# Planner costs, the places of twelve gates and one-bank accumulators in a two-layer hybrid backbone

## The chip, the core and the metric

One core of a Trainium2 chip runs the whole program: TensorE (PE, with its weight loads PEld), VectorE (DVE), ScalarE (ACT), GpSimd (POOL), and SyncE (SP), which issues the DMAs. The metric is the device time of one execution, in microseconds (us). All arithmetic that the result rests on is float32 or float32r; every large product is made of three float32r products.

## What is computed

The reference, cut to the parts that the change touches:

```python
for l in range(DEPTH):                                    # 2 layers, D_MODEL 1024
    h  = rms_norm(x)   * (1 + scale)   + shift            # 512 latent tokens
    hc = rms_norm(ctx) * (1 + scale_c) + shift_c          # 256 context tokens
    # one input projection feeds three mixers and the gates mg (3 x 1024 columns)
    y_gla  = head_norm_gate(bidir_recurrence(gla),  ga_g) # 4 heads, chunked scans
    y_hg   = head_norm_gate(bidir_recurrence(hgrn), hg_g) # 8 heads, chunked scans
    y_att  = window_attention(q, k, v, sink) * silu(wa_g) # 8 query heads, 2 kv heads
    merged = sum_n sigmoid(mg[n]) * (y[n] @ w_branch[n])  # n = gla, hg, att
    x      = x + gate * (merged @ w_out)
    # in layer 1 the context tokens go the same way; in layer 2 they only give k, v and states
return rms_norm(x)
```

## The kernel before

Tokens lie along the free dimension: 768 columns (512 latent, then 256 context), 128 channels to a tile. `hH` and `hL` hold the rounded and the remaining part of the normalised input. A **projection** (`proj_T`) takes one 128-column block of weights and makes 24 matmuls of 512 columns and, where context tokens are wanted, 24 of 256 into one accumulator; after its last matmul the caller evicts the accumulator (a copy, a SiLU, a sigmoid, a product). Accumulators come from a pool of two tiles of [128, 1024] floats, two banks each; small products use four one-bank tiles `mx`. `proj_V` makes token-major products, 6 groups of 24 matmuls of 256 columns, three groups to a tile.

Weights: `W` blocks are loaded by SP into three `raw` buffers, split into two parts by ACT or DVE into the ring `wring` (three blocks), up to two blocks ahead.

**What sets the order.** Each engine's order is written out by the program itself. `make_plan` lists the jobs: for each layer the GLA projections, the HGRN projections (`hf`, `hq`, `hg`, `hv`), the attention projections (`av`, `ak`, `aq`, `ag`), then the merge: gates `mg` (n, d), branch products `br` (n, d) and the output `out`. Between the matmuls of these jobs, at `pace()`, the recorder `Emit` fits in steps of **background generators**: `rec_head` (one head of a recurrence: scans on DVE, exps on ACT, transposes and small products on PE), `att_block` (scores, softmax, transposes, products for a block of 128 queries), `rope` and `yload_` (loads the finished rows `y` of a branch back from memory and splits them for `br`). `Emit` keeps a clock per engine from a cost formula per operation (`tt`, `stt`, `scan`, `act`, `copy`, ...) and a hop from engine to engine; `first` puts a step in when the clock says that its inputs are ready no later than 50 ns after PE's place, and `pace` goes on until DVE's or ACT's clock is 3 us ahead of PE's. `need` puts steps in until one generator is done, ready or not. `ACTIVE` bounds how many large generators of a kind are open; before, a generator that could not begin stopped all behind it in the queue (`runnable`).

A gate that is made early (`mgx`) is stored to memory and loaded again at `yneed`, just before its `br`. In layer 1 two gates are made early, in layer 2 eight (four ahead of the attention projections, two each in its third and fourth round).

The loads of `yload_`, of the weights and of early gates, and the stores of all outputs stand in one queue, SP's, in the order written.

The last job before the merge's first product is `yneed (0, ...)`: it loads the early gates and calls `need` for the two `yload_` generators of branch 0, each of four rows: three loads, the first split, the fourth load, three more splits.

## Time and profile before

| what | value |
| --- | --- |
| median of 3 runs (lowest to highest) | 2675.74 us (2675.12 to 2677.64) |
| the profiled execution, its own time | 2677.51 us |
| its span, first to last instruction | 2675.7 us |
| mean granted TensorE clock | 0.995 |
| PE busy | 2607.5 us, 97% |
| DVE, ACT, POOL busy | 1767.0, 1104.8, 169.3 us |
| PE idle (span less busy) | 68.2 us |

How to read it: PE works nearly all the time, so a gain is idle time of PE that goes away, or matmuls that run at the higher clock instead of the lower. Layer 1 goes from 0 to 1515 us (start to 55, GLA to 302, HGRN to 747, attention to 1035, merge from there), layer 2 from 1515 to the end (GLA to 1743, HGRN to 2106, attention to 2379, merge from there). In the rows below, `mx` and `acc` are PSUM tiles, `s` any of 40 slots, `s<-y` a load of a branch's rows, `y<-s` a store of them. The kernel's lines are named as L533 (matmul), L549 (transpose), L439 (activation), L450 (two-tensor operation), L470 (scan), L481 (copy on ACT).

### The profile page before, as it was taken

To read this page: it belongs to the slowest core of one execution; us is meant where nothing else is said; L and a number is where in the kernel's file an instruction comes from. 1 tells how busy PE (TensorE), PEld (TensorE's weight loads), DVE (VectorE), ACT (ScalarE), POOL (GpSimd) and SP (SyncE) were. 2 spreads that over 40 slices of the span, in tenths; PEclk is the share of its full clock that TensorE was granted. 3 is DMA by queue.
4 is the path that set the end of the run, shared out by engine and by line. 5 is a ranking of instruction groups with operands and counts; after the bars stand their busy time and mean duration, and the time that the engine had idled before them with its cause. 6 is when DMAs were issued, how large, how long until landed. Compare 5 with 4: busy or idle time off the path is not lost. (4 is left out here: it accounts for less than half of the span.)

```text
span 2675.7 us, 40576 instructions
## 1 busy us (share of the span) xinstructions
PE 2607.5 (97%) x15982; PEld 2314.4 (86%) x15982; DVE 1767.0 (66%) x3595; ACT 1104.8 (41%) x2034; POOL 169.3 (6%) x426
## 2 busy tenths in 40 slices
PE   8999999999999999999999999999999999999998
PEld 5999989989888888888888798888889797888886
DVE  5566657686777766774546556667887787664454
ACT  4444433444434455321211444445565545663222
POOL 0000002101010100000000000001011110000000
PEclk9999999999999999999999999999999999999999
DMA  7111211111111112553423311112121212224333
GB/s 262 56 52 60 60 60 50 58 46 62 50 53 49 54 58 76 173 193 95 142 95 105 132 50 61 65 62 64 61 68 60 76 56 78 70 93 137 132 124 106
DMA packets 89342, 227.68 MB, mean 85 GB/s; under 512 B 9920, under 2 KB 30912, under 8 KB 89152
## 3 DMA queue, kind: packets, MB, share of 16 engines
q1 hardware_dynamic: 89152, 225.09, 25.6%
q8 instruction: 126, 2.06, 0.3%
q14 instruction: 64, 0.52, 0.1%
HBM read 202.24 MB, written 22.81 MB: 84 GB/s over the span
## 5 line engine op out<-in xcount | busy, mean ns | idle before, releaser
L533 PE MATMUL acc<-hH,wring 128*128 128x512 f32 (+1 forms) x5040 | 1398.8, 356 | 14.6 <-ACT s L439 9.6
L533 PEld LDWEIGHTS acc<-hH,wring 128*128 128x128 f32 x5040 | 894.7, 189 | 141.5 <-ACT s L439 11.3
L533 PE MATMUL acc<-hL,wring 128*128 128x512 f32 (+1 forms) x2520 | 881.6, 351 | 3.6 <-DVE hL L466 3.5
L533 PEld LDWEIGHTS acc<-hL,wring 128*128 128x128 f32 x2520 | 477.2, 190 | 61.9 <-DVE hL L466 5.9
L533 PE MATMUL mx<-s,s 128*128 128x256 f32 (+4 forms) x2576 | 390.0, 299 | 12.8 <-DVE s L513 4.3
L533 PEld LDWEIGHTS mx<-s,s 128*128 128x128 f32 (+1 forms) x2576 | 348.9, 192 | 32.6 <-issue 7.0
L450 DVE TENSOR_TENSOR wring<-raw,wring 128x1024 fp32r<-128x1024 f32 x269 | 330.5, 1234 | 29.2 <-ACT wring L481 19.5
L533 PE MATMUL acc<-s,wring 128*128 128x512 f32 (+1 forms) x1728 | 332.3, 354 | 0.5 <-DVE s L450 0.5
L533 PEld LDWEIGHTS acc<-s,wring 128*128 128x128 f32 x1728 | 285.6, 189 | 46.3 <-DVE s L450 0.9
L439 ACT ACTIVATE s<-s 128x768 f32<-128x768 f32 (+1 forms) x321 | 259.0, 816 | 130.7 <-DVE s L466 83.1
L481 ACT CAST wring<-raw 128x1024 fp32r<-128x1024 f32 x173 | 179.7, 1047 | 276.9 <-PE acc L533 189.9
L533 PE MATMUL acc<-wring,hH 128*128 128x256 f32 x1536 | 286.1, 285 | 0.0
L450 DVE TENSOR_TENSOR s<-s,s 128x768 f32<-128x768 f32 (+5 forms) x279 | 234.2, 854 | 66.7 <-ACT s L439 46.5
L533 PEld LDWEIGHTS acc<-wring,hH 128*128 128x128 f32 x1536 | 242.2, 192 | 0.3
L533 PE MATMUL acc<-wring,hL 128*128 128x256 f32 x768 | 217.2, 283 | 0.0
L450 DVE TENSOR_TENSOR s<-s,fb 128x128 f32<-128x128 f32 (+2 forms) x608 | 182.8, 359 | 0.8
L439 ACT ACTIVATE s<-acc 128x768 f32<-128x768 f32 (+2 forms) x112 | 76.2, 683 | 254.5 <-PE acc L533 234.8
L481 ACT COPY s<-mx 128x256 f32<-128x256 f32 (+2 forms) x187 | 66.2, 379 | 207.4 <-PE mx L533 142.7
L479 DVE CAST wring<-raw 128x1024 fp32r<-128x1024 f32 x103 | 71.5, 694 | 118.0 <-PE acc L533 114.9
L533 PEld LDWEIGHTS acc<-wring,hL 128*128 128x128 f32 x768 | 147.3, 192 | 0.2
L481 ACT COPY s<-acc 128x768 f32<-128x768 f32 (+2 forms) x129 | 87.8, 680 | 98.2 <-PE acc L533 96.1
L549 PE MATMUL mx<-const,s 128*128 128x128 f32 (+1 forms) x732 | 109.6, 276 | 15.7 <-DVE s L450 14.6
(112 smaller groups left out, 2141.8 us busy)
## 6 DMA issues: line engine op xcount, KB each, us to landing
raw<-in_W SPq DMA_DIRECT2D x308, 512.0 KB, 3.8
y<-s SPq DMA_DIRECT2D x80, 128.0 KB, 1.7
s<-y SPq DMA_DIRECT2D x24, 384.0 KB, 6.2
s<-in_xT SPq DMA_DIRECT2D x16, 384.0 KB, 4.0
s<-in_wada SPq DMA_DIRECT2D x16, 384.0 KB, 7.5
s<-y SPq DMA_DIRECT2D x24, 256.0 KB, 4.4
y<-s SPq DMA_DIRECT2D x80, 64.0 KB, 1.6
s<-in_wvl SPq DMA_DIRECT2D x8, 288.0 KB, 6.1
```

Of the source, the lines that this page charges most:

```text
L439: self.nc.scalar.activation(out, in_, func, **kw)
L450: (self.nc.vector if e == 'v' else self.nc.gpsimd).tensor_tensor(out, a, b, op=op)
L479: self.nc.vector.tensor_copy(out, in_)
L481: self.nc.scalar.copy(out, in_)
L533: self.nc.tensor.matmul(out, lhsT=lhsT, rhs=rhs, start=start, stop=stop)
L549: self.nc.tensor.transpose(out, in_, ident)
```

## The change

1. **Costs of `Emit`.** A scan costs 2.05 n + 64 ns for n columns instead of 1.04 n + 65. An operation on DVE with a column operand costs 65 ns more. ACT's fixed part goes from 95 (70 for a copy) to 60 (50) from PSUM and 110 (90) from SBUF, and 90 more with a column as bias or scale. POOL's fixed part goes from 100 to 140.
2. **Accumulators.** The pool holds four tiles of [128, 512], one bank each. `proj_T` and `proj_V` take a tile for each part (512 latent, 256 context) and call an `evac` function inside, as soon as the part's last matmul is written, ahead of the last `pace()`. So each eviction with context becomes two.
3. **Gates.** `AT` and `EARLY` place the early gates. Layer 1: two, as before. Layer 2: twelve, namely (0, 0) to (0, 7) and (2, 7) to (2, 4): three inside HGRN (ahead of its rounds 2, 3, 4), four ahead of attention, four in its third and fourth round, one behind it.
4. **Queue.** In `runnable` a `yload_` that cannot begin no longer stops the others, nor they it; `box` is keyed by row.

```diff
+AT = (((0, 0, 0, 0), 0, (0, 0, 1, 1), 0), ((0, 1, 1, 1), 4, (0, 0, 2, 2), 1))
+EARLY = ([(0, d) for d in range(8)], [(0, d) for d in range(8)] + [(2, 7 - d) for d in range(8)])
...
+    def act_cost(self, out, in_, bias=None, scale=None):
+        return 0.833 * self.size(out) + (60 if self.psum(in_) else 110) + 90 * (self.is_ap(bias) or self.is_ap(scale))
...
-        self._do('a', 0.833 * self.size(out) + 95 + (90 if accum_out is not None else 0), out, [in_, bias, scale])
+        self._do('a', self.act_cost(out, in_, bias, scale) + (90 if accum_out is not None else 0), out, [in_, bias, scale])
...
         self.nc.vector.tensor_tensor_scan(out, d0, d1, 0.0, op0=ALU.mult, op1=ALU.add)
-        self._do('v', 1.04 * self.size(out) + 65, out, [d0, d1])
+        self._do('v', 2.05 * self.size(out) + 64, out, [d0, d1])
...
-    acc_p = es.enter_context(tc.tile_pool(name="acc", bufs=2, space=PSUM))
+    acc_p = es.enter_context(tc.tile_pool(name="acc", bufs=4, space=PSUM))
...
     def runnable():
         out = []
+        held = set()
         for b in queue:
-            if b.running:
+            if b.running or not b.begun and (b.name == 'y') in held:
                 continue
             if not b.begun:
-                if (b.need < 3 or sum(x.need > 2 for x in arena.active) < ACTIVE[b.name]) and \
-                        arena.spare() >= b.need - len(b.own):
-                    out.append(b)
-                break
+                held.add(b.name == 'y')
+                if b.need > 2 and sum(x.need > 2 for x in arena.active) >= ACTIVE[b.name] or \
+                        arena.spare() < b.need - len(b.own):
+                    continue
             out.append(b)
         return out
...
-    def proj_T(i, xH, xL, ctx, m=P):
-
-        ps = acc()
+    PARTS = ((0, NL), (NL, NC))
+
+    def proj_T(i, xH, xL, ctx, evac):
+
         E.t['pe'] = max(E.t['pe'], wready[i])
-        for t0, n in ((0, NL), (NL, NC)) if ctx else ((0, NL),):
+        for t0, n in PARTS[:2 if ctx else 1]:
+            ps = acc()[:, 0:n]
+            sl = slice(t0, t0 + n)
             k = 0
             for kt in range(KT):
                 for w, x in ((WH(i), xH), (WH(i), xL), (WL(i), xH)):
-                    mm(ps[0:m, t0:t0 + n], w[:, kt, 0:m], x[kt][:, t0:t0 + n],
-                       start=(k == 0), stop=(k == 3 * KT - 1))
+                    mm(ps, w[:, kt], x[kt][:, sl], start=(k == 0), stop=(k == 3 * KT - 1))
                     k += 1
                 if kt == 1 and t0 == 0:
                     ahead()
+                if kt == KT - 1:
+                    evac(sl, ps)
                 if kt % 2 == 1:
                     pace()
         pace()
-        return ps
```

Both programs hold 14,829 matmuls, of the same shapes; ACT's instructions go from 1,772 to 1,988, among them table loads from 104 to 147 and reads of PSUM from 784 to 939; DVE's go from 3,597 to 3,579, SP's DMAs from 620 to 628.

**Place 1, PE, layer 2, the third GLA head's V projection and the K projection after it.** The rows with `wring` ahead of `hH` are the V projection, those with `hH` ahead of `wring` the K projection; `mx<-const` are transposes of a head's decayed keys, which DVE makes. Before:

```order
L533 MATMUL acc_15069<-wring_85,hL7_84 128x256
L533 MATMUL acc_15069<-wring_85,hH7_76 128x256
L549 MATMUL mx_15156<-const_90,s767_15126 128x128 x3
L549 MATMUL mx_15161<-const_90,s767_15126 128x128 x2
L533 MATMUL acc_15167<-hH0_69,wring_85 128x512
```

Now (the rows left out are the same three for the second and third `hH`, `hL`):

```order
L552 MATMUL acc_15367<-wring_85,hL7_84 128x256
L552 MATMUL acc_15367<-wring_85,hH7_76 128x256
L552 MATMUL acc_15441<-hH0_69,wring_85 128x512
L552 MATMUL acc_15441<-hL0_77,wring_85 128x512
L552 MATMUL acc_15441<-hH0_69,wring_85 128x512
...
L552 MATMUL acc_15441<-hH3_72,wring_85 128x512
L552 MATMUL acc_15441<-hL3_80,wring_85 128x512
L552 MATMUL acc_15441<-hH3_72,wring_85 128x512
L568 MATMUL mx_15458<-const_90,s767_15434 128x128 x3
L568 MATMUL mx_15463<-const_90,s767_15434 128x128 x2
```

The transposes moved behind twelve matmuls of 512 columns.

**Place 2, SP, the end of layer 1's attention.** `y0_0_k` are the rows of branch 0 that the merge's first product needs, `y0_2_k` outputs of attention blocks, `raw` weights. Before, these stand in the job of the gate (0, 5), with the gates (0, 6) and (0, 7) still to come:

```order
L397 DMA s572_10634<-y0_0_3_157 128x768
L407 DMA y0_2_6_176<-s577_10657 128x128
L407 DMA y0_2_7_177<-s577_10657 128x128
L407 DMA y0_2_6_176<-s578_10669 128x128
L407 DMA y0_2_7_177<-s578_10669 128x128
L397 DMA s581_10684<-y0_0_4_158 128x768
L397 DMA s582_10686<-y0_0_5_159 128x768
```

Now they stand behind the last gate, in `yneed`:

```order
L423 DMA y0_2_6_176<-s572_10961 128x128
L423 DMA y0_2_7_177<-s572_10961 128x128
L413 DMA s573_10966<-y0_0_0_154 128x768
L413 DMA s574_10968<-y0_0_1_155 128x768
L413 DMA s575_10970<-y0_0_2_156 128x768
L413 DMA s578_10976<-y0_0_3_157 128x768
L423 DMA y0_2_6_176<-s587_11006 128x128
L423 DMA y0_2_7_177<-s587_11006 128x128
L413 DMA s588_11011<-y0_0_4_158 128x768
L413 DMA s589_11013<-y0_0_5_159 128x768
L413 DMA s590_11015<-y0_0_6_160 128x768
L413 DMA s593_11021<-y0_0_7_161 128x768
```

All eight loads moved behind the outputs of the last but one attention block, and four of them behind that of the last.

On PE the same place reads so now (`mx<-const` are the last block's transposes, `mx<-s585` its product, `acc<-s576` the merge's first product):

```order
L552 MATMUL mx_10945<-s564_10873,s336_7233 128x256
L568 MATMUL mx_10990<-const_90,s568_10919 128x128
L568 MATMUL mx_10990<-const_90,s569_10922 128x128
L568 MATMUL mx_10990<-const_90,s568_10919 128x128
L568 MATMUL mx_10990<-const_90,s569_10922 128x128
L552 MATMUL mx_10999<-s585_10995,s334_7231 128x256
L552 MATMUL mx_10999<-s586_10996,s334_7231 128x256
...
L552 MATMUL acc_11041<-s576_10972,wring_85 128x512
L552 MATMUL acc_11041<-s577_10973,wring_85 128x512
L552 MATMUL acc_11041<-s576_10972,wring_85 128x512
```

No matmul of a gate is left between the last attention block and the merge's first product.

**Place 3, ACT, layer 1, the gate (0, 0) in the middle of attention.** `sm<-nsink` and the activations of 256 columns beside it are a softmax. Before:

```order
L439 ACT_TABLE_LOAD
L439 ACTIVATE s_9065<-acc 128x768
L481 CAST wring<-raw_8755 128x1024
L481 CAST s_9085<-mx 128x512
L421 ACT_TABLE_LOAD
L439 ACTIVATE sm<-nsink,sm 128x1
```

Now:

```order
L458 ACT_TABLE_LOAD
L458 ACTIVATE s_9017<-acc 128x512
L437 ACT_TABLE_LOAD
L458 ACTIVATE sm<-nsink,sm 128x1
L458 ACTIVATE s_9042,sm<-mx,sm 128x256 x2
L458 ACTIVATE sm<-nsink,sm 128x1
L458 ACTIVATE s_9046,sm<-mx,sm 128x256 x2
L458 ACTIVATE s_9046<-s_9046,sm 128x512
L458 ACT_TABLE_LOAD
L458 ACTIVATE s_9017<-acc 128x256
L437 ACT_TABLE_LOAD
```

The gate's eviction moved apart into two, with a softmax and two table loads between them.

## Rows read from the trace of the kernel before

**Rows 1.** Page, part 1: busy us, share of the span, instructions.
```profile
PE 2607.5 (97%) x15982; PEld 2314.4 (86%) x15982; DVE 1767.0 (66%) x3595; ACT 1104.8 (41%) x2034; POOL 169.3 (6%) x426
```

**Rows 2.** Stretches of the span: busy us of each engine (instructions), clock, DMA, GB/s.
```profile
0.00:100.00 100.00, 89.54 (x592) 70.19 (x593) 52.12 (x110) 43.23 (x66) 0.20 (x4) 0.98 0.53 191
...
1000.00:1100.00 100.00, 98.89 (x662) 89.64 (x659) 62.68 (x143) 54.86 (x123) 0.00 (x0) 1.00 0.30 96
...
2100.00:2200.00 100.00, 96.25 (x639) 86.72 (x638) 80.17 (x199) 44.49 (x98) 12.18 (x35) 0.98 0.20 65
...
2600.00:2700.00 100.00, 64.91 (x282) 52.47 (x280) 37.04 (x49) 15.64 (x19) 0.00 (x0) 0.96 0.23 79
```

**Rows 3.** Waits of PE on accumulators: us in total, times, longest.
```profile
PE acc L533 <- ACT s L439: 9.6, 5, 3.9
...
PE acc L533 <- ACT s L481: 3.0, 2, 1.6
...
PE acc L533 <- DVE s L466: 1.8, 1, 1.8
```

**Rows 4.** PE groups by shape: busy us, mean ns, idle before them, what ended it.
```profile
L533 PE MATMUL mx<-s,s 128*128 128x256 f32 x1200 | 200.5, 317 | 2.2 <-ACT s L439 1.6 <-DVE s L450 0.6
L533 PE MATMUL mx<-s,s 128*128 128x128 f32 x1248 | 162.1, 277 | 10.5 <-DVE s L513 4.3 <-DVE s L479 3.4 <-ACT s L481 2.7
L549 PE MATMUL mx<-const,s 128*128 128x128 f32 x720 | 108.0, 276 | 15.7 <-DVE s L450 14.6 <-ACT s L439 0.5 <-DVE s L462 0.5
```

**Rows 5.** Timeline, DVE and PE, third GLA head of layer 2: start, us, instruction, count.
```profile
1631.11 3.52 DVE L470 TENSOR_TENSOR_SCAN s<-scm,s 128x384 f32<-128x384 f32 x4
...
1645.07 0.74 PE L549 MATMUL mx<-const,s 128*128 128x128 f32 x5 [1.56 <-DVE s L450]
```

**Rows 6.** Timeline, ACT and PE, layer 2's attention, two SiLU evictions behind a softmax.
```profile
2256.31 0.29 ACT L439 ACTIVATE sm<-nsink,sm 128x1 f32<-128x1 f32 x1 [8.57 <-DVE sm L450]
...
2260.15 1.28 ACT L439 ACT_TABLE_LOAD   x1
2261.44 1.09 ACT L439 ACTIVATE s<-acc 128x512 f32<-128x512 f32 x2
...
2262.09 0.50 PE L533 MATMUL acc<-hH,wring 128*128 128x512 f32 x1 [3.94 <-ACT s L439]
```

**Rows 7.** Short stretches of PE: us, busy (matmuls), granted clock, DMA.
```profile
2262.64:2266.06 3.42, 3.42 (x13) 0.50 0.45 153
2266.06:2269.48 3.42, 3.42 (x26) 1.00 0.09 23
...
2444.34:2449.78 5.44, 5.44 (x25) 1.00 0.97 347
```

**Rows 8.** Timeline, end of layer 1's attention: SP's DMAs, splits on ACT and DVE, PE.
```profile
1082.77 1.93 SPq L397 DMA_DIRECT2D s<-y  x4
1091.60 1.74 SPq L407 DMA_DIRECT2D y<-s  x4
1093.44 1.79 SPq L397 DMA_DIRECT2D s<-y  x4
...
1087.13 0.83 ACT L481 CAST s<-s 128x768 fp32r<-128x768 f32 x1 [1.20 <-DMA s<-y]
...
1096.47 0.83 ACT L481 CAST s<-s 128x768 fp32r<-128x768 f32 x1 [5.16 <-DMA s<-y]
...
1092.08 0.94 DVE L450 TENSOR_TENSOR s<-s,s 128x768 fp32r<-128x768 f32 x1
...
1103.19 0.95 DVE L450 TENSOR_TENSOR s<-s,s 128x768 fp32r<-128x768 f32 x1
...
1101.13 0.50 PE L533 MATMUL acc<-hH,wring 128*128 128x512 f32 x1 [2.25 <-ACT s L439]
```

**Rows 9.** ACT's groups: table loads of one of two lines; splits of weights.
```profile
L439 ACT ACT_TABLE_LOAD x53 | 68.0, 1283 | 5.0 <-PE acc L533 3.4 <-PEq L1846 0.7
...
L481 ACT CAST wring<-raw 128x1024 fp32r<-128x1024 f32 x173 | 179.7, 1047 | 276.9 <-PE acc L533 189.9
```

More of the change, by code (lines that the diff above doesn't have):

```diff
@@ L115, in make_plan @@
             job(l, 'grun', h)
+        early = EARLY[l][:sum(sum(x) if isinstance(x, tuple) else x for x in AT[l])]
+        spilled = set(early)
         for p in range(4):
+            for _ in range(AT[l][0][p]):
+                mgx(l, early.pop(0))
             todo = []
@@ L127, in make_plan @@
             job(l, 'hrun', p)
-        early = [(0, d) for d in range(2 if ctx else 8)]
-        spilled = set(early)
-        if not ctx:
-            for _ in range(4):
-                mgx(l, early.pop(0))
+        for _ in range(AT[l][1]):
+            mgx(l, early.pop(0))
         v = False
@@ L144, in make_plan @@
                 job(l, 'aq', h, win('wa_q', h))
-            for _ in range(0 if p < 2 else 1 if ctx else 2):
+            for _ in range(AT[l][2][p]):
                 mgx(l, early.pop(0))
@@ L149, in make_plan @@
             job(l, 'arun', p)
+        for _ in range(AT[l][3]):
+            mgx(l, early.pop(0))
+        assert not early
         cond = [(l, i) for i in range(16, 24)] + [(l + 1, i) for i in range(24)] if ctx else []
@@ L487, in affine @@
         n = self.size(out)
-        cost = {'v': (1.04 if psum else 0.52) * n + 65, 'a': 0.833 * n + 95}
+        cost = {'v': (1.04 if psum else 0.52) * n + 130, 'a': self.act_cost(out, in_, bias)}
         e = self._pick({k: c for k, c in cost.items() if k in eng}, out, [in_])
@@ L496, in scale @@
         n = self.size(out)
-        cost = {'v': 0.52 * n + 65, 'a': 0.833 * n + 95}
+        cost = {'v': 0.52 * n + 130, 'a': self.act_cost(out, in_, None, s)}
         if self._pick({k: c for k, c in cost.items() if k in eng}, out, [in_, s]) == 'v':
@@ L1212, in logsig_gla, with rope, evac @@
         return bg(rest(), 1, 'sig', soon=True)
-    def rope(ps, H, L, ctx, factor=None):
-        w, u = arena.alloc(NL), arena.alloc(NL)
-        for g in range(0, P, 32):
-            copy(u.ap[g ^ 32:(g ^ 32) + 32], ps[g:g + 32, 0:NL], eng='va', psum=True)
-        if factor is None:
-            tt(w.ap, ps[:, 0:NL], cosT, ALU.mult)
-        else:
-            stt(w.ap, ps[:, 0:NL], factor, cosT, ALU.mult, ALU.mult)
-        if ctx and factor is None:
-            E.split(H[:, NL:NT], L[:, NL:NT], ps[:, NL:NT], psum=True)
-        elif ctx:
-            act(H[:, NL:NT], ps[:, NL:NT], AF.Copy, scale=factor)
-            stt(L[:, NL:NT], ps[:, NL:NT], factor, H[:, NL:NT].bitcast(F32), ALU.mult, ALU.subtract)
+    def rope(ctx, factor=None):
+        i = take()
+        n = NT if ctx else NL
+        got = []
+        def evac(sl, ps):
+            if sl.start == 0:
+                got.extend([arena.alloc(n, True), arena.alloc(n, True), arena.alloc(NL), arena.alloc(NL)])
+                w, u = got[2:]
+                for g in range(0, P, 32):
+                    copy(u.ap[g ^ 32:(g ^ 32) + 32], ps[g:g + 32], eng='va', psum=True)
+                if factor is None:
+                    tt(w.ap, ps, cosT, ALU.mult)
+                else:
+                    stt(w.ap, ps, factor, cosT, ALU.mult, ALU.mult)
+            elif factor is None:
+                E.split(got[0].r[:, sl], got[1].r[:, sl], ps, psum=True)
+            else:
+                act(got[0].r[:, sl], ps, AF.Copy, scale=factor)
+                stt(got[1].r[:, sl], ps, factor, got[0].ap[:, sl], ALU.mult, ALU.subtract)
+        proj_T(i, hH, hL, ctx, evac)
+        a, b, w, u = got
+        H, L = a.r, b.r
         def rest():
@@ L1336, in att_block, with project, evac @@
         finish()
-    def silu_evac(ps, n):
-        b = arena.alloc(n)
-        act(b.ap, ps[:, 0:n], AF.Silu)
-        return b
+    def project(ctx, func=None, scale=None):
+        i = take()
+        out = []
+        def evac(sl, ps):
+            if not out:
+                out.append(arena.alloc(NT if ctx else NL))
+            if func is None:
+                copy(out[0].ap[:, sl], ps, eng='va', psum=True)
+            else:
+                act(out[0].ap[:, sl], ps, func, scale=scale)
+        proj_T(i, hH, hL, ctx, evac)
+        return out[0]
     def tok(bufs, w, c, o=0, r=False):
@@ L1459, in j_start @@
             i = take(2)
-        ps = [acc(), acc()]
         parts = [((0, NL), (NL, NC)), ((0, NL), (NL, NC))[:2 if S_['ctx'] else 1]]
+        ps = [[acc()[:, 0:n] for _, n in x] for x in parts]
         def products(kt, of=(0, 1), js=(0, 1)):
@@ L1765, in j_out, with evac @@
             load_v(l + 1)
-        ps = proj_T(take(), hH, hL, ctx)
+        i = take()
         if ctx and d > 3:
             split_v()
-        if d == 7:
-            E.table(COMBINED)
-            S0['sq'].close()
-        for j, (t0, m) in enumerate(((0, NL), (NL, NC))[:2 if ctx else 1]):
-            stt(xr.ap[:, t0:t0 + m], ps[:, t0:t0 + m], ada[l][:, 16 + d, j:j + 1], xr.ap[:, t0:t0 + m],
-                ALU.mult, ALU.add)
+        def evac(sl, ps):
+            j = int(sl.start > 0)
+            if d == 7:
+                E.table(COMBINED)
+                S0['sq'].close()
+            stt(xr.ap[:, sl], ps, ada[l][:, 16 + d, j:j + 1], xr.ap[:, sl], ALU.mult, ALU.add)
+        proj_T(i, hH, hL, ctx, evac)
         S0['sq'].add(xr.ap)
```

114 lines of the change are left out of this document (53 added, 61 removed).

## The prediction

> **What bounds the kernel now.** I read the engines' shares first: PE is busy for 2607.5 of 2675.7 us [rows 1], so 68.2 us of idle PE and whatever the clock withholds are all that can be won, as both programs hold the same 14,829 matmuls. Then I split the idle time. The table by stretches gives the two ends [rows 2]: the first 100 us lack 10.5 and the last 75.7 lack 10.8; there PE waits for first loads and for the last norm, which the change leaves alone. The list of PE's waits gives the accumulators [rows 3]: 9.6 + 3.0 + 1.8 = 14.4 us in eight waits, where a projection waits until ACT or DVE has emptied its tile. The PE groups by shape give the background work [rows 4]: 15.7 + 10.5 + 2.2 = 28.4 us ahead of transposes and small products of heads and attention blocks. Some 4 us more lie at the change of layers and in small gaps.
>
> The clock hides a further cost. After a long wait the granted clock falls to 0.50, 1.2 instead of 2.4 GHz, for 3.42 us, in which 13 matmuls run where the next 3.42 us hold 26 of the same mix [rows 7]: 1.7 us lost, counted as busy. There are five such stretches between the ends (at 941.7, 1102.1, 1535.6, 2136.4, 2262.6 us), of which the last stands in the rows.
>
> **Part 1: accumulators.** The longest wait shows the cause. Two SiLU evictions of layer 2 stand on ACT behind a softmax that itself waited 8.57 us for DVE; PE, two projections ahead, has no tile left and waits 3.94 us [rows 6]. A projection without context is 24 matmuls of 512 columns, 5.44 us [rows 7], and takes one bank: four tiles let PE run 16 us ahead of the oldest eviction instead of 5.4. With context the depth stays at two projections, but the eviction of the latent part is written 24 matmuls earlier. The largest wait is 3.94 us, so I take all 14.4 as gone except the 2.25 at 1101 us [rows 8], which I count in part 4: **-12.2**. If a freed PE runs into the next late chain, a third comes back: bound -8.
>
> **Part 2: scan costs and the waits of background work.** The four long scans of a head take 3.52 us, 0.88 each [rows 5]; the old formula gives 0.46 for 384 columns, the new one 0.85. So the planner's DVE clock was 1.6 us early per head, and the transposes behind them wait 1.56 us [rows 5]. That agreement is why I trust this part. Place 1 shows the repair: the transposes now stand behind twelve more matmuls, 12 x 0.227 = 2.7 us, and DVE's chain is no longer than it was. I compared, for all 35 waits of this kind, how many matmuls stand between the step that makes the input and the one that reads it: at 27, with 16.7 of 28.4 us, they grew by at least the wait; at three more, the GLA heads of layer 2 as in place 1 (4.7 us), the reader itself moved back. The rest mostly grew a little. I take **-24** (bounds -17, the 27 alone, to -28.4).
>
> **Part 3: the clock.** Four of the five slow stretches follow waits that parts 1 and 2 remove (941.7, 1535.6, 2136.4, 2262.6): 4 x 1.7 = **-6.8**; half of it if shorter waits still bring the clock down.
>
> **Part 4: the end of layer 1's attention, a new wait.** Evictions in halves interleave with softmaxes (place 3), so ACT's table loads go from 104 to 147 and reads of PSUM from 784 to 939. A load takes 1.283 us [rows 9]: 43 x 1.283 = 55 us more for ACT, and with some 0.2 us for each added read about 30 more: 1104.8 + 85 = 1190 us, 45% of the span, no bound by itself. But 31 of the 43 fall in layer 1 (counted in ACT's order), and a planner that sees DVE and ACT as fuller puts less in per gate. The result is place 2: the loads of branch 0's rows used to stand two gates ahead of the merge; now they stand behind the last gate.
>
> I follow that chain with the rows of before [rows 8]. On SP the loads of rows 0 to 3 stand behind the store of the last but one block's output, so they start when PE has made that output. In before such a pass of four loads took from 1082.77 to 1093.02 us until the fourth was split, 10.2 us; with 4.4 us to the first split (1087.13) and four splits of 0.95 alone it would be 8.2. Meanwhile PE has the last block's transposes (0.4 us) and then waits, because DVE's split of those transposes stands behind the four splits of rows: with 0.9 us for two stores and 0.7 for that split, a first wait of 9 to 11 us; I take 10. Then the last block's product, its store, and only then loads 4 to 7: 3.0 us to the first split (1093.44 to 1096.47) and 6.8 to 10.7 to the end of the last. PE covers the time with the merge's first product, 8 steps of 0.68 us, but its fifth step needs row 4: a second wait of 3.5 to 7.3; I take 5. Less the 2.25 us that stood at this place, plus one more slow stretch of the clock: 15 - 2.25 + 1.7 = **+14.5** (bounds +3, if the loads run well ahead of what I see, to +20). The weights of this stage are loaded ahead of it, so I add no wait for them.
>
> Layer 2 has the same pattern with one gate, 5.44 us, and half the rows still to come, so its second pass is covered.
>
> **Part 5: the rest.** Twelve early gates cost four stores and four loads more on SP, at 0.43 us of issue each [rows 8]; weights wait for the ring, not the reverse: 189.9 us of the idle time ahead of their splits is waiting for PE [rows 9]. So nothing for the DMAs. The moved gates are matmuls that PE makes in any case; what they are worth is in parts 1 and 2, as work to fit the chains into. Opening the queue for loads changes nothing where they now wait for free slots. For new small waits, the table loads within chains above all, I add **+2** (0 to +6). The start, the end and the 2.9 us at the change of layers stay.
>
> **Sum.** -12.2 - 24 - 6.8 + 14.5 + 2 = -26.5 from the profiled execution's 2677.5: 2651.0. That execution lies 1.8 above the median of 2675.7, so I forecast 2649 us.
>
> **A rule against the change.** Where a softmax is followed by an eviction, ACT ends one instruction at 2260.14, loads its table from 2260.15 for 1.28 us and starts the next at 2261.44 [rows 6]: a switch costs 1.29 us, with nothing around it. The Trainium skill, page "ScalarE: Activation LUTs", section "What ACT_TABLE_LOAD costs", puts every switch at 2.66 us, 1.28 for the load and 1.38 for a drain, and asks for one set to be finished before the next is begun, which this change does the contrary of. The load agrees with the row, the drain is not to be seen. By the page's price the 43 switches would be an estimated 114 us of ACT instead of 55.
>
> **Rivals.**
>
> *Slower: the table loads lie in chains.* Each added load stands between the halves of an eviction and a softmax or a head's exps. If PE waited for every one of them, 43 x 1.283 = 55 us come on top: 2704. It decides from 21 loads (27 us) on. For it: ACT is at 54.9% in 1000 to 1100 us already [rows 2], where the most are added. Against: the planner counts each load at 1.28, and PE has tiles for two projections meanwhile. Chance 0.07. By the page's price this case would be an estimated 2763.
>
> *No change: the chains are the bound and the waits only move.* In 2100 to 2200 us DVE is at 80.2% [rows 2]; were it the limit, PE would run into the background waits later and as long. Part 2 and half of part 3 fall away: -12.2 - 3.4 + 14.5 + 2 = +0.9, so 2677. The same comes about if the change doesn't do what it says, that is, if the truer scan costs don't move the readers of the other heads as at place 1. Against both: the 1.56 us that equal the scan error, and 27 of 35 places. Chance 0.11.
>
> *The end of layer 1 is cheaper.* If the loads land as fast as in before's second pass and DVE has nothing else to do, part 4 is +3 to +5: 2638 to 2640. Against: two store-to-load passes in a row stand in the order. Chance 0.20.
>
> **How the numbers follow.** Forecast 0.62, its own range 2641 to 2661 (part 2 between its bounds); cheaper end 0.20; no change 0.11; slower 0.07. The bounds of all parts together give 2630 to 2674; with no more than 2 in 10 left out I give 2634 to 2668. A measurement of this kernel can tell about 0.2% (5.4 us) from no change. Faster by more: the forecast and the cheaper end, 0.82, less 0.01 for its upper tail: 0.81. Within 0.2%: 0.11. Slower: 0.08.
>
> **What would show it.** In the profile after: waits of PE on accumulators below 2 us in sum; the transposes' 15.7 us below 4; slow stretches of the clock at the layer's end and the change of layers, hardly elsewhere; between the last gate and the first product of layer 1 two waits, about 10 us ahead of a small product and 5 inside the first merge product, behind `s<-y` DMAs. Part 4 is wrong if that place is short; part 2 if many waits of 1 to 2 us stand ahead of transposes again; the first rival is right if chains of ACT with table loads end PE's waits.

## The result

The changed kernel takes **2647.4 us** (median of 4 runs, 2643.8 to 2647.5) against 2676.2 for the kernel before on the same chip (2675.1 to 2677.6): a ratio of 0.9886, 95% interval 0.9871 to 0.9902, 28.8 us faster. The forecast was 2649 us. The profiled execution took 2647.5 us, its span 2645.7, to be set beside the 2677.5 and 2675.7 of before.

### The profile after

Part 1 of the page, which answers to [rows 1], then PE's waits, which answer to [rows 3] (us in total, times, longest):

```profile
PE 2600.5 (98%) x15982; PEld 2314.4 (87%) x15982; DVE 1734.7 (66%) x3577; ACT 1205.9 (46%) x2250; POOL 175.2 (7%) x431
```

```profile
PE mx L552 <- ACT s L500: 10.2, 2, 9.1
PE mx L568 <- DVE s L469: 5.3, 4, 3.0
...
PE acc L552 <- DVE hL L485: 3.2, 4, 1.8
PE acc L552 <- ACT hH L458: 1.9, 1, 1.9
...
PE acc L552 <- ACT s L500: 1.7, 1, 1.7
PE acc L552 <- POOL s L469: 1.4, 1, 1.4
```

The span fell by 30.0 us: PE's idle time by 23.0 (68.2 to 45.2) and its busy time by 7.0. Where an accumulator waited for the eviction of a projection (the three rows of [rows 3], 14.4 us) nothing is left: the `acc` rows above wait for the normalised input `hH` and `hL`, at the start and at the change of layers, or for the rows of a branch in the merge. The longest wait, 9.1 us, is new.

PE's groups by shape, which answer to [rows 4] (busy us, mean ns, idle before them):

```profile
L552 PE MATMUL mx<-s,s 128*128 128x256 f32 x1200 | 202.2, 318 | 10.1 <-ACT s L500 9.1 <-DVE s L469 0.8
L552 PE MATMUL mx<-s,s 128*128 128x128 f32 x1248 | 160.3, 275 | 0.9 <-DVE s L532 0.9
L568 PE MATMUL mx<-const,s 128*128 128x128 f32 x720 | 105.7, 273 | 6.6 <-DVE s L469 5.3 <-ACT s L500 0.6 <-DVE s L481 0.6
```

The 28.4 us of background waits are 17.6 now, of which 10.2 lie at the end of layer 1's attention; elsewhere 7.4 remain. That end, [rows 8] before, looks like this on PE, DVE, ACT and SP (start, us, instruction, idle before it and its releaser):

```profile
1086.61 0.67 PE L568 MATMUL mx<-const,s 128*128 128x128 f32 x4 [0.55 <-DVE s L481]
1096.41 0.58 PE L552 MATMUL mx<-s,s 128*128 128x256 f32 x1 [9.14 <-ACT s L500]
...
1098.75 4.86 PE L552 MATMUL acc<-s,wring 128*128 128x512 f32 x12
1105.30 0.51 PE L552 MATMUL acc<-s,wring 128*128 128x512 f32 x1 [1.70 <-ACT s L500]
1107.19 3.35 PE L552 MATMUL acc<-s,wring 128*128 128x512 f32 x7 [1.38 <-POOL s L469]
...
1091.91 0.56 DVE L498 CAST s<-s 128x768 fp32r<-128x768 f32 x1 [5.05 <-DMA s<-y]
...
1096.78 0.68 DVE L469 TENSOR_TENSOR s<-mx,s 128x512 fp32r<-128x512 f32 x1
...
1094.13 1.74 ACT L500 CAST s<-s 128x768 fp32r<-128x768 f32 x2 [5.76 <-DMA s<-y]
1095.78 0.58 ACT L500 CAST s<-mx 128x512 fp32r<-128x512 f32 x1
...
1087.17 0.86 SPq L423 DMA_DIRECT2D y<-s  x2
1088.14 1.91 SPq L413 DMA_DIRECT2D s<-y  x4
1099.30 0.80 SPq L423 DMA_DIRECT2D y<-s  x2
1100.20 1.79 SPq L413 DMA_DIRECT2D s<-y  x4
```

PE makes the last block's four transposes at 1086.6. ACT and DVE split them only at 1095.8 and 1096.8, because ahead of them stand the splits of branch 0's rows (`s<-s` 128x768), and those wait for loads that SP issued only at 1088.1, behind a store (1087.2). PE waits 9.1 us with nothing else to do, then makes the last product, and only behind its store (1099.3) do loads 4 to 7 start. Five waits together: 0.55 + 9.14 + 0.53 + 1.70 + 1.38 = 13.3 us. The clock fell with it (stretch, us, busy us and matmuls of PE, granted clock, DMA):

```profile
1089.34:1103.00 13.66, 6.07 (x17) 0.50 0.54 182
1106.30:1113.10 6.80, 5.91 (x16) 0.50 0.62 253
1512.50:1515.90 3.40, 3.32 (x8) 0.50 0.00 0
2321.50:2324.90 3.40, 3.40 (x18) 0.50 0.00 0
```

At 0.50, 1.2 GHz, PE was busy for 12.0 us at this place (the first two rows); at twice the clock, by [rows 7], the same matmuls would take some 6.0. So the place costs an estimated 13.3 + 6.0 = 19.3 us. The other two slow stretches stand at the change of layers and behind a 3.0 us wait in layer 2's attention.

### The profile page after: what moved, and what is told of

Same layout as the page of the kernel before. It is cut to its first block, busy times and chain, and to the rows that moved or that the text cites. A ratio compares the mean times of both kernels' runs of the same rounds, so it can differ in the third digit from the quotient of the medians.

```text
span 2645.7 us, 40826 instructions
## 1 busy us (share of the span) xinstructions
PE 2600.5 (98%) x15982; PEld 2314.4 (87%) x15982; DVE 1734.7 (66%) x3577; ACT 1205.9 (46%) x2250; POOL 175.2 (7%) x431
## 4 chain that ended last, share of the span: by engine, by line
PE 91%; DVE 5%; ACT 2%; DMA 2%; issue 1%; SPq 0%; POOL 0%; DVEq 0%; ACTq 0%
PE acc L552 73%; PE mx L552 14%; PE mx L568 3%; DVE s L469 2%; DVE s L485 1%; ACT s L458 1%; DMA s<-y 1%; DMA raw<-in_W 1%; ACT s L500 1%; DVE wring L469 0%; DVE hL L485 0%; DMA s<-in_xT 0%; SPq L413 0%; DVE sm L536 0%; PE mx L564 0%
## 5 line engine op out<-in xcount | busy, mean ns | idle before, releaser
L552 PE MATMUL acc<-s,wring 128*128 128x512 f32 (+1 forms) x1728 | 337.7, 358 | 3.7 <-ACT s L500 1.7
L458 ACT ACTIVATE s<-s 128x768 f32<-128x768 f32 (+1 forms) x321 | 258.9, 816 | 126.6 <-DVE s L485 83.1
L500 ACT CAST wring<-raw 128x1024 fp32r<-128x1024 f32 x186 | 193.1, 1047 | 259.0 <-PE acc L552 184.5
L469 DVE TENSOR_TENSOR s<-s,s 128x768 f32<-128x768 f32 (+4 forms) x275 | 230.8, 858 | 60.1 <-ACT s L458 38.3
L458 ACT ACTIVATE s<-acc 128x512 f32<-128x512 f32 (+2 forms) x164 | 84.3, 519 | 234.1 <-PE acc L552 232.7
L500 ACT COPY s<-acc 128x512 f32<-128x512 f32 (+2 forms) x197 | 96.7, 499 | 168.6 <-PE acc L552 167.6
L498 DVE CAST wring<-raw 128x1024 fp32r<-128x1024 f32 x90 | 61.8, 687 | 89.8 <-PE acc L552 85.4
L469 DVE TENSOR_TENSOR s<-s,acc 128x512 f32<-128x512 f32 x72 | 42.3, 596 | 111.5 <-PE acc L552 111.4
```

The lines of the kernel that those rows point to most:

```text
L458: self.nc.scalar.activation(out, in_, func, **kw)
L469: (self.nc.vector if e == 'v' else self.nc.gpsimd).tensor_tensor(out, a, b, op=op)
L498: self.nc.vector.tensor_copy(out, in_)
L500: self.nc.scalar.copy(out, in_)
L552: self.nc.tensor.matmul(out, lhsT=lhsT, rhs=rhs, start=start, stop=stop)
```

## Experiments

Each was compared with the kernel before on the same chip (2675.8 to 2677.0 us). "Gain" is the difference of these medians; the intervals of the ratios are about 0.0013 to either side, 3.5 us, so two experiments differ clearly from some 5 us on. The questions: do costs, accumulators and gates each earn what the prediction gave them, and what makes the wait at the end of layer 1?

### The new costs alone

```diff
 # the kernel before, with the planner's costs of the changed one, for instance
-        self._do('v', 1.04 * self.size(out) + 65, out, [d0, d1])
+        self._do('v', 2.05 * self.size(out) + 64, out, [d0, d1])
...
-    cost = {'v': (1.04 if psum else 0.52) * n + 65, 'a': 0.833 * n + 70, 'g': 3.34 * n + 260}
+    cost = {'v': (1.04 if psum else 0.52) * n + 65, 'a': 0.833 * n + (50 if self.psum(in_) else 90), 'g': 3.34 * n + 260}
```

> The kernel before with the new planner costs alone; accumulators of two tiles, gates and queue as before. My theory (two separate gains): the background waits of 28.4 us shrink by 17 to 24 as in the changed kernel, the accumulator waits of 14.4 us stay, and since the loads of branch 0's rows still stand one and a half gates ahead of the merge, the end of layer 1's attention costs no more than before (2 to 4 us). Two of the four slow stretches of the clock go (-3.4). That gives 2648 to 2657 us, about 2652. Rival A (the costs do nothing without tiles, because the evictions hold everything up): 2670 to 2677. Rival B (truer costs alone bring the new wait at the end of layer 1): 2660 to 2668, with 10 us or more of waits of PE just ahead of the merge's first product.

2661.3 us, ratio 0.9941 (0.9928 to 0.9953), a gain of 15.7. PE's waits:

```profile
PE acc L544 <- ACT s L450: 13.0, 6, 3.5
...
PE mx L544 <- DVE s L524: 5.8, 6, 1.8
```

As expected the accumulators' waits stay and the end of layer 1 has none, so truer costs alone don't bring the new wait. Rival A, which gave the costs nothing, falls. The time lies 4 us above my range and inside rival B's, but the wait that rival B needs is not there; background waits, two groups of 3.4 us at HGRN pairs of layer 2 among them, shrank less than I thought.

### The accumulators alone

```diff
 # the kernel before with these, and evictions in parts
-    acc_p = es.enter_context(tc.tile_pool(name="acc", bufs=2, space=PSUM))
+    acc_p = es.enter_context(tc.tile_pool(name="acc", bufs=4, space=PSUM))
...
-        return ps_tile('acc', acc_p, [P, 1024], 2)
+        return ps_tile('acc', acc_p, [P, 512], 4)
```

> The changed kernel with the planner's costs, the early gates and the queue of the kernel before: what is left of the change is the one-bank accumulators and the evictions in parts. My theory: the accumulator waits go (-10 to -12), two slow stretches of the clock with them (-3.4), the background waits stay or grow somewhat with 10 more table loads (0 to +8): 2661 to 2668 us, about 2664. By the cause that I gave for the end of layer 1 (evictions in halves alone bring table loads and push the loads of rows behind the last gate) 13 us of waits would stand there and the time would be 2674 to 2680; as the loads of rows stand a whole gate ahead of the merge in this order, I now expect that place at 0 to 4 us.

2664.2 us, ratio 0.9948 (0.9936 to 0.9961), a gain of 12.8, on the expected 2664. The transposes' waits are there as before, and at the end of layer 1 stand two waits of 3.3 us in sum, of which this is the long one:

```profile
PE mx L557 <- DVE s L458: 15.5, 20, 2.0
```

```profile
1090.25 0.38 PE L541 MATMUL mx<-s,s 128*128 128x256 f32 x1 [2.92 <-ACT s L489]
```

So evictions in parts alone don't make the 13.3 us wait either, contrary to the cause that the prediction gave.

### The old gates in the changed kernel

```diff
-AT = (((0, 0, 0, 0), 0, (0, 0, 1, 1), 0), ((0, 1, 1, 1), 4, (0, 0, 2, 2), 1))
+AT = (((0, 0, 0, 0), 0, (0, 0, 1, 1), 0), ((0, 0, 0, 0), 4, (0, 0, 2, 2), 0))
```

> The changed kernel with layer 2's early gates where they were before: four ahead of the attention's keys and two each in its third and fourth blocks, none between the heads' pairs. Layer 1 is the same instruction for instruction. My theory (gates are worth nothing by themselves): 2645 to 2651 us, within 0.2% of the changed kernel. Rival (the gates are what covers the waits of layer 2's HGRN pairs): waits of PE in 1800 to 2400 us grow by 6 us or more, 2653 to 2665.

2670.0 us, ratio 0.9974 (0.9964 to 0.9984): the gain shrinks from 28.8 to 7.0. My expectation falls, and the rival's time was too small. PE's waits between 1900 and 2450 us are 24.2 us (7.9 in the changed kernel); first its longest rows, then PE's busy time and clock in two of the places, of this kernel and then of the changed one:

```profile
PE mx L552 <- ACT s L500: 4.9, 2, 4.5
PE mx L568 <- ACT s L458: 3.9, 1, 3.9
...
PE acc L552 <- ACT s L500: 3.2, 1, 3.2
```

```profile
2110.00:2140.00 30.00, 20.94 (x118) 0.77 0.04 14
2310.00:2330.00 20.00, 14.70 (x94) 0.74 0.05 14
```

```profile
2110.00:2140.00 30.00, 30.00 (x182) 1.00 0.33 108
2310.00:2330.00 20.00, 16.68 (x105) 0.91 0.14 43
```

In the first place, where the attention begins, PE is full at 2.4 GHz in the changed kernel; with the old gates it waits, and the clock falls as well. In the second, in the third block, the changed kernel still waits 3.0 us, but less than this one.

### The old cost of a scan in the changed kernel

```diff
-        self._do('v', 2.05 * self.size(out) + 64, out, [d0, d1])
+        self._do('v', 1.04 * self.size(out) + 65, out, [d0, d1])
```

> The changed kernel with one number put back: the planner's cost of a scan (0.46 instead of 0.85 us for 384 columns). My theory (the scan is the term that keeps the transposes from waiting): the waits ahead of the heads' transposes return, 4 scans x 0.4 = 1.6 us in those heads whose transposes are due early, 8 to 16 us in sum; at the end of layer 1 the loads of rows move ahead of part of the last gate and the 13.3 us of waits there shrink to 3 to 9; so 2643 to 2655 us, with the two effects told apart by the list of PE's waits. Rival (other costs did the work): background waits outside the end of layer 1 stay near 7.4 us.

2652.4 us, ratio 0.9907 (0.9893 to 0.9921): 5 us slower than the changed kernel, at the limit of what can be told. Waits return, but not where the theory put them. In 60 to 1070 us, where the changed kernel has no wait, 9.6 us return (3.0, 2.0, 2.0, 1.3, 1.1, 0.2): 4.4 of them at HGRN heads, up to 790 us, and 5.2 in attention blocks. The end of layer 1 has 4.3 us of waits instead of 13.3. So this one number earns some 10 us and gives most of it back at the end of layer 1.

At place 1, on which the prediction built, the wait of 1.56 us [rows 5] does not return. The same transposes with the old cost of a scan alone, and then with all the old costs (the second kernel under "Costs and gates, and accumulators and gates"):

```profile
1641.19 0.74 PE L568 MATMUL mx<-const,s 128*128 128x128 f32 x5 [0.29 <-DVE s L469]
```

```profile
1638.64 0.74 PE L557 MATMUL mx<-const,s 128*128 128x128 f32 x5 [0.94 <-DVE s L458]
```

With the scan's old cost alone they still stand behind matmuls of the K projection; with all the old costs they stand right behind the V projection again. So at this place the other costs are enough to move the reader.

### The new gates alone

```diff
 # the kernel before, with
+AT = (((0, 0, 0, 0), 0, (0, 0, 1, 1), 0), ((0, 1, 1, 1), 4, (0, 0, 2, 2), 1))
```

> The kernel before with the early gates of layer 2 alone: twelve instead of eight, at the new places; old costs, two accumulator tiles. In the experiment that put the gates back the time rose by 22.6 us, so gates cover chains of layer 2. My theory now (gates are matmuls that stand between a head pair's steps, and work whatever the tiles and costs are): background waits in 1800 to 2450 us shrink by 5 to 10 us, accumulator waits stay at about 14: 2664 to 2672 us. Rival (gates need the four tiles: with two, each gate's eviction holds PE up as much as the gate covers): 2674 to 2682.

2672.8 us, ratio 0.9982 (0.9973 to 0.9992), a gain of 4.2, just above the theory's range. The background waits did not shrink: 29.5 us, 28.4 before, and in 1800 to 2450 us, which the theory named, 10.2 against 9.0; PE's waits ahead of `acc` fell from 17.8 to 14.2 (the two ends left out). So what the theory named did not happen.

### Costs and gates, and accumulators and gates

```diff
 # first: the kernel before, with the new costs and
+AT = (((0, 0, 0, 0), 0, (0, 0, 1, 1), 0), ((0, 1, 1, 1), 4, (0, 0, 2, 2), 1))
 # second: the changed kernel, with the old costs, for instance
-        self._do('v', 2.05 * self.size(out) + 64, out, [d0, d1])
+        self._do('v', 1.04 * self.size(out) + 65, out, [d0, d1])
```

> The kernel before with the new costs and the new gates, without the one-bank accumulators. With costs alone the time was 2661.3 us, with 13 us of waits at two HGRN pairs of layer 2 (3.4 each), and at the merge's start (3.5), beside 13 us on accumulators. My theory now (gates cover background chains, tiles cover evictions, and only the parts together with truer costs push the loads of rows at the end of layer 1): the waits at the HGRN pairs and at the merge's start go, the accumulators' stay, layer 1's end stays free of waits: 2648 to 2655 us. Rival (gates need the tiles): 2659 to 2665. If it comes out below the changed kernel's 2647.4, the accumulators cost more at the end of layer 1 than they bring elsewhere.

2659.5 us, ratio 0.9930 (0.9917 to 0.9942): the rival's range. PE's waits ahead of `acc` are 20.2 us (17.8 in the kernel before by the same count), 11.9 of them behind ACT (L458), the longest 4.4: with two tiles the gates add nothing measurable to the costs (17.5 against 15.7).

> The changed kernel with the planner's old costs (accumulators, evictions in parts, gates and queue as changed). Banks alone gave 2664.2 us. My theory: the scan waits of about 1.0 to 1.6 us ahead of the heads' transposes stay in both layers (some 10 us), the 5.3 us at layer 2's merge and 2 us at an HGRN pair are covered by gates, the end of layer 1 stays at 3.3 us instead of 13.3: 2651 to 2659 us. If costs and gates are worth their sum over banks (-15.7 - 22.6) it would be 2642: I expect it not to be.

2657.0 us, ratio 0.9923 (0.9910 to 0.9935), within the expected range and far from the sum. The end of layer 1 has 3.2 us of waits.

The eight combinations, as gains over the kernel before in us (the small change to the queue goes with the accumulators wherever these stand with another part):

| | old gates | new gates | gates' part |
|---|---|---|---|
| neither | 0 | 4.2 | 4.2 |
| costs | 15.7 | 17.5 | 1.8 |
| accumulators | 12.8 | 20.0 | 7.2 |
| both | 7.0 | 28.8 | 21.8 |

With the old gates, costs and accumulators together gain less than either alone. The gates' parts of 4.2 and 1.8 are within what two runs can differ by.

### Two gates ahead of the merge in layer 1

```diff
-            steps = [(0, [(0, d) for d in range(8)], range(8)), (1, [(1, d) for d in range(4)], range(4)),
+            steps = [(0, [(0, d) for d in range(8)] + [(1, 0), (1, 1)], range(8)), (1, [(1, d) for d in range(4)], range(4)),
```

> The changed kernel with one edit at the end of layer 1: two gates of the merge's second branch are made before its first product instead of after it, so that 16 us more of matmuls stand between the loads of branch 0's rows and the product that reads them. My theory (the 13.3 us of waits there are the time from store over load and split to the product, and have no cover): they shrink to 0 to 3 us, the slow clock there goes too (about 5 us), nothing else changes: 2628 to 2634 us. Rival (ACT or DVE is late there, not the loads; then the waits stay whatever PE does meanwhile): 2643 to 2649.

2634.9 us, ratio 0.9838 (0.9825 to 0.9852), 12.5 below the changed kernel and just above the expected range. The waits at the place fall from 13.3 to 5.5, all of it at the last block's product, and this the long one:

```profile
1089.96 0.58 PE L552 MATMUL mx<-s,s 128*128 128x256 f32 x1 [5.02 <-ACT s L500]
```

The waits inside the merge's first product are gone, so they lacked cover; the first wait is shorter but still there, so cover was not all that it lacked.

### The parts of a gate's eviction together

```diff
 # in proj_T, for SiLU and sigmoid
-                if kt == KT - 1:
-                    evac(sl, ps)
+                if kt == KT - 1 and (t0 > 0 or not ctx or not together):
+                    for h in held:
+                        evac(*h)
+                    held.clear()
```

> The changed kernel with one edit: the two parts of a SiLU's or sigmoid's eviction are written one after the other, behind the second part, instead of each behind its own. ACT's table loads fall from 147 to 124. By the cause in my prediction (interleaved halves bring table loads, and these push the loads of rows behind the last gate) the end of layer 1 gets shorter, 13.3 us of waits down to 6 or less: 2636 to 2641 us. Rival (table loads are not the cause; the planner places that stage by what it believes of the loads' time): in this order all eight loads of rows stand behind the last block's store, so PE waits once, 6 to 10 us, ahead of the merge's first product: 2642 to 2650.

2638.3 us, ratio 0.9857 (0.9842 to 0.9872). The time is the first theory's, the place is the rival's: the loads of rows still stand behind the last gate, in one pass behind the last store, and PE waits once ahead of the merge's first product.

```profile
PE acc L552 <- ACT s L500: 5.2, 1, 5.2
PE mx L552 <- DVE s L469: 1.6, 1, 1.6
```

With two smaller ones (1.1 and 0.2 us) these are 8.2 us instead of 13.3. With 23 table loads fewer the loads didn't move ahead: the number of table loads is not shown to place them.

### The planner knows that SP issues in order

```diff
     def load(self, out, in_):
-        t = max([self.t['d'], self.free_at.get(n, 0.0), self.written.get(in_.tensor.name, 0.0)]
+        t = max([self.t['d'], self.sp, self.free_at.get(n, 0.0), self.written.get(in_.tensor.name, 0.0)]
...
     def store(self, out, in_):
-        self.written[out.tensor.name] = max(self.t['d'], self.written.get(in_.tensor.name, 0.0)) + 2500.0
+        self.sp = max(self.sp, self.written.get(in_.tensor.name, 0.0))
+        self.written[out.tensor.name] = max(self.t['d'], self.sp) + 2500.0
```

> The changed kernel with one edit in the planner alone: it now knows that SP issues its DMAs in order, so that a load that is written behind a store starts no earlier than what that store waits for. The order of instructions changes in few places; at the end of layer 1 the split of the last block's transposes stands ahead of the splits of the rows, and the last block's store ahead of load 3. My theory (the 9.1 us wait is the transposes' split standing on ACT and DVE behind splits whose loads the planner believed landed): that wait falls to 0 to 2 us, the wait ahead of the merge's first product grows from 3.1 to 4 to 7, and half of the slow clock goes: 2638 to 2643 us. Rival (the place is bound by the loads from the store on, however the splits stand): 12 to 14 us of waits stay, 2645 to 2649.

2639.6 us, ratio 0.9861 (0.9844 to 0.9877), 7.8 below the changed kernel. PE, DVE and SP at the place:

```profile
1086.71 0.39 PE L554 MATMUL mx<-s,s 128*128 128x256 f32 x1 [0.78 <-DVE s L500]
...
1091.07 0.80 PE L554 MATMUL acc<-s,wring 128*128 128x512 f32 x1 [2.35 <-DVE s L500]
...
1099.35 0.79 PE L554 MATMUL acc<-s,wring 128*128 128x512 f32 x1 [4.09 <-ACT s L502]
...
1085.96 0.69 DVE L500 CAST s<-mx 128x512 fp32r<-128x512 f32 x1 [0.46 <-PE mx L570]
...
1089.96 2.38 SPq L414 DMA_DIRECT2D s<-y  x5
```

The transposes are now split at 1085.96, at once, and the 9.1 us wait is 0.8. What is left stands ahead of the merge's first product (2.35 us), which begins with no cover, and inside it (4.09 us and small ones).

### Both edits

```diff
 # the two edits above: sp in load and store, and
+            steps = [(0, [(0, d) for d in range(8)] + [(1, 0), (1, 1)], range(8)), ...
```

> Both edits: the planner knows SP's order, and two gates of the merge's second branch stand ahead of the first product in layer 1. With the two gates alone 5.5 us of waits were left there, ahead of the last block's output, behind the splits of rows. My theory: these go too, and with them 1.7 to 3.4 us of slow clock: 2625 to 2630 us. Rival (they only move to the merge's first product): 2632 to 2636.

**2625.8 us**, ratio 0.9809 (0.9794 to 0.9823): 21.6 below the changed kernel, 51.0 below the one before, faster than both. PE, at 1075 to 1110 us, of the changed kernel and of this one:

```profile
1075.00:1110.00 35.00, 21.70 (x111) 0.75 0.49 168
```

```profile
1075.00:1110.00 35.00, 35.00 (x214) 1.00 0.64 218
```

No wait of PE and no slow clock is left there. So the end of layer 1 cost the changed kernel about 21.6 us, against 19.3 read from its trace. The two agree: in the profiles PE takes 363.1 and 343.2 us from its 7000th to its 9000th matmul, 19.9 us apart, and the two executions already stand 2.0 us apart at the 400th, far ahead of the place.

### Eight gates at the new places

```diff
 # on top of both edits
-AT = (((0, 0, 0, 0), 0, (0, 0, 1, 1), 0), ((0, 1, 1, 1), 4, (0, 0, 2, 2), 1))
+AT = (((0, 0, 0, 0), 0, (0, 0, 1, 1), 0), ((0, 1, 1, 1), 0, (0, 0, 2, 2), 1))
```

> The previous kernel (2625.8 us, no wait left at the end of layer 1) with eight early gates in layer 2, as many as in the kernel before, but at the new places: one ahead of each of the last three HGRN pairs, two each in the third and fourth attention blocks, one behind the last; the four ahead of the attention's keys are left out. With the old eight places the changed kernel had waits of 4.6 us at an HGRN pair (1970), 8.9 us where the attention begins (2118 to 2137), 5.3 us in its third block (2317) and 4.0 us at the merge's start (2437), 22.6 us with the slow clock. My theory (it is the place that counts: each gate covers the chain beside it): the waits where the attention begins return, 5 to 9 us with 2 to 4 us of slow clock, the others stay away: 2632 to 2640 us. Rival A (the number counts, since fewer gates leave less for PE to do everywhere): 2642 to 2650. Rival B (the four are idle cover): 2624 to 2629.

2643.9 us, ratio 0.9882 (0.9866 to 0.9899): 18.1 us lost with four gates fewer, above my range and in rival A's. Three of PE's rows tell where:

```profile
2097.65 1.62 PE L554 MATMUL mx<-s,s 128*128 128x128 f32 x6 [2.20 <-DVE s L534]
...
2109.46 0.90 PE L570 MATMUL mx<-const,s 128*128 128x128 f32 x3 [6.86 <-DVE s L471]
...
2405.55 2.80 PE L554 MATMUL acc<-s,wring 128*128 128x512 f32 x5 [4.66 <-DVE s L500]
```

The first two are the waits that the theory named; the waits at the HGRN pair (1970) and in the third block (2317) stayed away, as it said. The third it did not foresee: at layer 2's merge the first product now stands right behind the last block's, without cover, the same pattern as in layer 1. The three waits are 13.7 us, and PE's waits between the two ends grew by no more than 11.3 (10.6 to 21.9), so rival A's cause, less for PE to do everywhere, is not what the rows show. Place counts, and so does that enough gates are left for each place.

## Why the prediction was right, and where it was not

**The sum.** -26.5 us was forecast from the profiled execution, -30.0 came. The terms agree less well than the sum. Over parts 3 and 4 the clock was to give back 6.8 - 1.7 = 5.1 us; it cost 0.9 more than before. PE's busy time, which no part priced, fell by 7.0 us in spite of that and filled the gap. That the sum lies so near is in part luck.

**Part 1, accumulators: right.** -12.2; the rows of evictions are gone, the 2.25 us that part 4 counts among them. The accumulators alone gain 12.8, and with two tiles the waits stay whatever else is changed (costs and gates: 20.2 us).

**Part 2, background waits: size about right, cause too narrow.** -24 was forecast, 28.4 - 7.4 = 21.0 went; the transposes' 15.7 us fell to 6.6, not below 4. The step gave it to the scan cost, and to the readers that moved behind more matmuls. Three things show that it was more. The scan's number alone is worth some 10 us of waits, and the agreement of 1.56 with 1.6 us at place 1, for which the prediction trusted this part, doesn't make the scan the cause: with the scan's old cost alone the wait there is 0.29 us. In layer 1, whose gates did not change, PE's background waits between 60 and 1060 us were 14.4 us before, 8.2 with the new costs alone, 12.6 with the accumulators alone and none with both. And in the changed kernel with the old gates PE's list of waits has 30.9 - 10.5 = 20.4 us of background waits outside the end of layer 1, where by the same count the changed kernel has 7.9: some 12 are the gates'. The prediction had counted the matmuls between writer and reader with the gates in place, so its size held, but it never priced the gates: part 5 says that what they are worth "is in parts 1 and 2, as work to fit the chains into", and without them 22 us go.

**Part 3, the clock: wrong.** -6.8 was forecast. The four named stretches went with their waits (941.7, 1535.6, 2136.4, 2262.6), but two others came, at 1512.5 and at 2321.5, behind waits of 1.92 and 3.0 us. The first of these waits, for the normalised input, stood in the kernel before as well, and no slow stretch followed it there (PE's row, and the stretch around it with its clock):

```profile
1515.74 0.49 PE L533 MATMUL acc<-hH,wring 128*128 128x512 f32 x1 [1.92 <-ACT hH L439]
```

```profile
1510.00:1520.00 10.00, 7.62 (x43) 1.00 0.36 118
```

So a wait that stays can bring a slow stretch that was not there before, and a count of stretches by the waits that go is unsafe. With 12.0 us of busy time at 0.50 at the end of layer 1 and 6.7 at the other two, 9.4 us are lost to the clock between the ends, before 5 x 1.7 = 8.5. The larger miss is "one more slow stretch" in part 4: with the one that stood there before it makes 6.8 us of slow clock, and the trace has 20.5, of which 6.6 lie behind the end of the 9.1 us wait (1096.4 to 1103.0) and 6.8 more begin at the two waits inside the merge's first product.

**Part 4, the end of layer 1: place, shape and first wait right, cause wrong.** Forecast were a first wait of 10 and a second of 5 us (3.5 to 7.3) behind `s<-y` DMAs; measured are 10.2 and 3.1, the second below its bounds. With the clock the place costs 19.3 us by the trace and 21.6 by the last but one experiment; less the 2.25 and 1.7 that stood there before, 15.4 to 17.7 against +14.5. Counted between PE's 7000th and 9500th matmul of the two profiles, 437.1 us before and 450.4 after, it is 13.3. The price held, the slow clock making up for the shorter waits. That the transposes' split would stand behind the splits of rows was read rightly from the order. The cause that the prediction gave for that order was a chain: halves, so table loads, so less background per gate, so late loads of rows. Halves without the costs gave 3.3 us there, costs without the halves none, and 23 table loads fewer left the loads where they were. Shown is this: the wait needs costs and halves together; its long part goes when the planner knows that a load stands on SP behind a store, and the rest when two gates stand ahead of the merge. The planner took the rows as landed while SP still waited to issue them, and so wrote their splits on DVE and ACT ahead of the split that PE needed. Why just this pair of edits drives the loads behind the last gate is not settled. The fourth part of the change, the queue, which is about these loads, is in every kernel that shows the long wait, and no such kernel was run without it, so its share is not measured. Two things speak against it: with queue and accumulators but the old costs the place has only 3.2 us of waits, and the changed kernel's program written without the queue's part, which was not run, has its DMAs on SP in the same order.

**Rivals.** Table loads in chains, 2704: ACT rose to 1205.9 us (1190 forecast) with 147 loads of 1283 ns, and PE waits for none that the rows show. The rule weighed in the prediction (the Trainium skill, "ScalarE: Activation LUTs", "What ACT_TABLE_LOAD costs") asks 2.66 us for a switch; in the trace after, ACT ends an instruction at 1086.67, its load at 1086.69 takes 1.28 us and the next instruction starts at 1087.98, 1.29 us later, so the measurement decides against the drain, as in [rows 6]:

```profile
1086.16 0.51 ACT L458 ACTIVATE s<-s,sm 128x256 f32<-128x256 f32 x1 [0.49 <-DVE sm L547]
1086.69 1.28 ACT L458 ACT_TABLE_LOAD   x1
1087.98 0.38 ACT L458 ACTIVATE s<-acc 128x256 f32<-128x256 f32 x1
```

The advice to finish one set before the next is begun, which the prediction quotes with it, stands on the same page under "Table sets: the hidden batching unit".

"No change" falls with part 2, "cheaper end" with the 13.3 us.

## What to carry to other kernels

When several edits go into a planner, count the cover that each leaves for its neighbours: here costs and accumulators gained 15.7 and 12.8 us alone and 7.0 together, and the rest came only with gates moved beside the exposed chains. A planner's estimate of a load must include the queue that issues it; a split that waits for a load which stands behind a store holds up everything that is written behind that split on its engine. Price a long wait of PE with the slow clock behind it, which here added some 6 us to 13. When one number fits one wait, put that number back alone before you trust the fit: here 0.29 of 1.56 us returned.

## What the runs showed that was not expected

PE's busy time fell by 7.0 us with the same matmuls and no less slow clock. The mean of single shapes fell: transposes from 276 ns in [rows 4] to 273 above, and the low-rank projection of 288 columns, before and after:

```profile
L533 PE MATMUL acc<-s,hH 128*128 128x288 f32 x192 | 40.2, 303 | 1.7 <-ACT s L481 1.6
```

```profile
L552 PE MATMUL acc<-s,hH 128*128 128x288 f32 x192 | 38.8, 295 | 0.0
```

These two groups make up 2.3 + 1.4 of the 7.0 us; the rest is not traced to any shape. The ends of matmuls are modelled in the profile, so part of PE's busy time may be short waiting that the model hides and that goes with the waits that are shown. No run separates it, so this cause is not shown.

Costs and accumulators gain 7.0 us together, and 21.6 more were to be had at the end of layer 1: 28.6, which is the sum of what they gain alone, 28.5. That the loss there is their whole interplay would fit, but the 21.6 were measured with the new gates and with two gates of cover that the other kernels lack, the kernel with both edits and the old gates was not run, and the agreement may be chance.
